# A mixture of experts in blocks: the order of the weight loads, one weight buffer, and where the shared expert's down products stand

## The chip, the cores and the metric

The kernel runs as one program on one core of a Trainium2 chip. The metric is device microseconds from the start of an execution to its end, as the median of several executions. One execution was also profiled; all rows below come from that one.

## The reference, cut to what matters

Two transformer blocks follow each other on 512 tokens of width 1024, in float32. The first block ends in a mixture of experts, and this is where the change lies. Each token goes to 6 of 64 routed experts and also through one shared expert. The result is added to the residual, which the second block norms and projects.

```python
def moe_ffn(h, w_router, b_router, w_exp_gate, w_exp_up, w_exp_down, w_sh_gate, w_sh_up, w_sh_down):
    ...
    def expert_block(xs):
        tok, g, e = xs
        xb = x_pad[tok]
        hb = jax.nn.silu(xb @ w_exp_gate[e]) * (xb @ w_exp_up[e])
        return (hb @ w_exp_down[e]) * g[:, None]
    ...
    shared = (jax.nn.silu(xf @ w_sh_gate) * (xf @ w_sh_up)) @ w_sh_down
    return (shared + routed).reshape(B, S, D)
...
x = x + gate_f * moe_ffn(...)
return rms_norm(x, g_final)        # first_block; second_block begins with rms_norm_2(x, norm_mix) @ w_in
```

A routed expert has three matrices of 1 MB each: gate and up (1024 x 256) and down (256 x 1024). So the 64 experts are 192 MB in all, read once.

## The kernel before, in words

The residual stands in SBUF as `xres` (`xr`), four chunks of 128 tokens. `phase_b` computes the experts. It packs the 64 experts into 32 blocks of 128 token slots (`NB` = 32). A block holds one expert (128 slots), two (96 and 32, or 64 and 64), or three (64, 32, 32); `KINDS` lists the kinds, and `seq` is the order in which blocks are computed. Before the change, counted from block 0, the experts per block in that order are 2 2 2 2 2 3 1 2 2 2 2 3 1 2 2 2 2 3 1 2 2 2 2 3 1 2 2 2 2 3 1 2. The first two blocks (`STAT`) hold fixed experts, whose weights are loaded before the routing is known; the other 60 experts are loaded by an id that the routing gives.

One block is computed in these steps. `expert_h` multiplies the gathered tokens by gate and up on TensorE (PE), and ScalarE (ACT) and VectorE (DVE) make the hidden values `hs` of it (the ACT instruction is at L1011, one for each block). Then the next block's tokens are transposed (`slots_T`, L994), `combine` adds the block before to the residual by products with a selection matrix (L1054, L1055 on PE, the add L1056 on DVE), and `expert_out` multiplies the hidden values by the down matrix (L1033). All blocks cost PE the same, since experts that share a block run beside each other in the array. An optional `slot_info` in some blocks prepares indices of later blocks. Every matrix product of PE on plain float32 stands in the trace as two instructions. GpSimd (POOL) gathers the tokens of the block three further on.

The weights come through SyncE's (SP's) queue. Gate and up go into buffers of 1 MB that hold half of one expert's gate and up (`gu`): 3 named `rawh`, 6 named `raw`, 2 named `rawl`, and as a twelfth one `raws` (`last`), which at first holds the shared expert's down matrix `wd`. The down matrix goes into 8 buffers of 512 KB (`whi`, `wlo`, `rawd`). A buffer is free again when `expert_h` (gate and up) or `expert_out` (down) of its block is through. Each load is a piece of 512 KB: two for a gate-and-up half, one for a half of a down matrix. SP works its queue in order, so a load that waits for a buffer holds back all that stand behind it.

The order of SP's queue is a list that Python writes out, `stream`. `free` is the step at which a load's buffer comes free (step 2i is the end of `expert_h` of block i, step 2i+1 the end of its `expert_out`). Before the change, loads are sorted by `free`, then by the step that needs them.

The shared expert's hidden values `hsT` are made before the loop. Its down products are 4 chunks of tokens, each of 4 products (8 instructions on PE, L1409) and 2 adds on DVE (L1410). Before the change, chunk c stands in block c (`down_at`), ahead of that block's `combine`. When chunk 3 is through, `raws` serves as the twelfth weight buffer.

After the loop, `tail` adds the last two blocks to the residual for chunks 0 and 1, norms these rows (L1449 to L1462), transposes them (L1467), and does the same with chunks 2 and 3. The product of the second block that comes first, `nsa_kv`, multiplies the normed rows by 396 columns of `w_in`. Its matrix is split into high and low parts in four steps `q`, with 3 buffers for each part. Much of the order of instructions on each engine is set by a scheduler, except where `self.chain` or `self.order` ties PE's instructions to each other.

Of the kernel before, what the change touches and what calls it, by code (L numbers as in the profile page):

```python
# [17 lines left out]
OP = mybir.AluOpType  # L18
AX = mybir.AxisListType

T, D, NCH = 512, 1024, 4
KC = D // 128
# [36 lines left out]
class Kern:  # L59
# [861 lines left out]

    def gu(self, h):
        self.turn += 1
        n = self.NP + self.NX + self.NY
        t = self.turn if self.turn < n else (self.turn - n) % (n + 1)
        if t < self.NP:
            return self.hold.tile([128, self.RAW], F32, name="rawh", bufs=self.NP)
        if t < self.NP + self.NX:
            return self.raw(2048)
        return self.spare() if t < n else self.last()  # L930

    def last(self):
        return self.rp.tile([128, self.RAW], F32, name="raws")
# [124 lines left out]
    def phase_b(self):  # L1058
        nc, tc, I = self.nc, self.tc, self.I
        xr, hT, hp = self.xres, self.h2T, self.hp  # L1060
# [6 lines left out]
        wd = self.last().rearrange("p (k n) -> p k n", k=2)  # L1067
# [34 lines left out]
        hsT = rt.tile([128, 2, T], F32, name="hsT")  # L1102
# [11 lines left out]
        for j in range(3):  # L1114
            t = rt.tile([128, D], F32, name=f"xg{j}")
# [5 lines left out]
        p = 0  # L1121
# [75 lines left out]
        p = 0  # L1197
# [6 lines left out]
        for name, src in (("pos", pos), ("gate", sco)):  # L1204
            t = self.tps()
# [4 lines left out]
            t = self.tps()  # L1210
# [58 lines left out]
        seq = ks[0][:]  # L1269
        for i, p in enumerate(ks[2] + ks[3] + ks[5]):  # L1270
            seq.append(p)
            if i % 4 == 2:
                seq += [ks[4].pop(0), ks[1].pop(0)]
        assert sorted(seq) == list(range(NB))


# [1 line left out]
        n = 2  # L1278
# [7 lines left out]

        stream, ngu, ndn = [], self.NP + self.NX + self.NY, self.NHI + self.NLO + self.ND
        ug, ud = [], []  # L1290
        for i, p in enumerate(seq):
            es = self.experts(p)
            for h in range(2):
                for j in es:
                    t = len(ug)
                    free = -1 if t < ngu else 2 * ug[t - ngu] if t < 2 * ngu else 7 if t == 2 * ngu else 2 * ug[t - ngu - 1]
                    ug.append(i)
                    if i >= STAT:
                        stream.append((free, 2 * i, len(stream), p, j, h))
            for j in es:  # L1300
                for k in range(2):
                    t = len(ud)
                    free = -1 if t < ndn else 2 * ud[t - ndn] + 1
                    ud.append(i)
                    if i >= STAT:
                        stream.append((free, 2 * i + 1, len(stream), p, j, 2 + k))
        last = {0: -1, 1: -1}
        for n, (free, *r) in enumerate(stream):
            last[r[-1] > 1] = free = max(free, last[r[-1] > 1])
            stream[n] = (free, *r)  # L1310
        stream.sort()
        ids_of = {}

        def issue(now):

            while stream and stream[0][0] <= now:
                _, _, _, p, j, h = stream.pop(0)
                if (p, j) not in ids_of:
                    ld, (e,) = nc.values_load_multi_w_load_instructions(
                        ids[0:1, j * NB + p:j * NB + p + 1], engines=[mybir.EngineType.SP], min_val=0, max_val=E - 1)  # L1320
                    if len(ends) > 2:
                        self.order(ends[-3], ld[0])
                    ids_of[p, j] = e
                e, w = ids_of[p, j], loads.setdefault(p, {}).setdefault(j, [None] * 4)
                if h < 2:
                    w[h] = self.load_gu(self.gu(h), dyn, e, h)
                else:
                    w[h] = self.load_down(self.down(h - 2), dyn, e, h - 2)
                    ends.append(self.last_load)

        down_at = {0: [0], 1: [1], 2: [2], 3: [3]}
        ends, done = [], []
        fixed_down(1, 1)
        issue(-1)
# [2 lines left out]
                self.run(info(bs))  # L1337
        self.gather(xgs[2], tok[:, seq[2]:seq[2] + 1])
        xT = self.slots_T(xgs[0])
        def overflow():  # L1340

            xo = self.hold.tile([128, self.RAW], F32, name="rawh", bufs=self.NP)
            go, od = [self.spare() for _ in range(2)], self.last()
            more = nc.values_load(late[0:1, n2:], min_val=0, max_val=n2)
            with tc.If(more > 0):
                with tc.For_i(0, more) as q:
                    j = nc.values_load(late[0:1, ds(q, 1)], min_val=0, max_val=n2 - 1)
                    c4 = ep.tile([128, NCH], F32, name="c4")
                    p4 = ep.tile([128, NCH, 6], BF, name="p4")
                    lj = ep.tile([128, 1], F32, name="lj")  # L1350
                    nc.vector.tensor_copy(lj, lim2[:, ds(j, 1)])
                    nc.vector.tensor_copy(c4, slot[:, :, ds(j, 1)].rearrange("p c o -> p (c o)"))
                    nc.vector.tensor_scalar(c4, c4, lj, None, op0=OP.subtract)
                    nc.vector.tensor_copy(p4, pay[:, :, ds(j, 1), :].rearrange("p c o f -> p (c o) f"))
                    ne = nc.values_load(cnt[0:1, ds(j, 1)], min_val=-T, max_val=T)
                    e = nc.values_load(ids[0:1, ds(j, 1)], min_val=0, max_val=E - 1)
                    for b in range(NCH):
                        with tc.If(ne > 128 * b):
                            if b:
                                nc.vector.tensor_scalar(c4, c4, -128.0, None, op0=OP.add)  # L1360
                            o1 = ep.tile([128, 1], I32, name="o_tok")
                            o2 = ep.tile([128, 1], F32, name="o_tokf")
                            o3 = ep.tile([128, 1], F32, name="o_gate")
                            self.run(self.slot_info(ep, 1, [(0, 128, c4[:, :, None], lambda c, j: p4[:, c, :])], (o1, o2, o3)))
                            xg = xo[:, :D]
                            nc.gpsimd.memset(xg, 0.0)
                            self.gather(xg, o1)
                            xT = self.slots_T(xg)
                            w = [self.load_gu(go[h], dyn, e, h) for h in range(2)]
                            w += [self.load_down(od[:, k * D:(k + 1) * D], dyn, e, k) for k in range(2)]  # L1370
                            parts = [(0, 128, w)]
                            hs = self.expert_h(parts, xT, o3, "ho")
                            self.combine([(self.pick(o2), self.expert_out(parts, self.hidden_T(hs)))])
# [9 lines left out]
        for i, p in enumerate(seq):  # L1383
# [16 lines left out]
            if i + 1 < NB:  # L1400
                xT = self.slots_T(xgs[(i + 1) % 3])
                if i + 1 >= NB - 1:
                    nxt = up(xT, seq[i + 1])
            for c in down_at.get(i, []):
                for n in range(2):
                    pd = self.acc()
                    s = slice(n * 512, (n + 1) * 512)
                    for k in range(2):
                        self.pe(nc.tensor.matmul(pd, hsT[:, k, c * 128:(c + 1) * 128], wd[:, k, s], start=(k == 0), stop=(k == 1)))  # L1409
                    nc.vector.tensor_tensor(xr[:, c, s], xr[:, c, s], pd, op=OP.add)  # L1410
            y = None
            if i == NB - 1:
                y = self.hold.tile([128, self.RAW], F32, name="rawh", bufs=self.NP).bitcast(F32R)
# [4 lines left out]
            if done and i < NB - 1:  # L1418
                self.combine(done, range(2, NCH))
                done = []  # L1420
            done.append((self.pick(tokf[:, p:p + 1]), self.expert_out(parts, hT, y)))
            for g in infos:
                self.run(g)
            issue(2 * i + 1)
        self.chain = None
        assert not stream
        g = self.hold.tile([128, self.RAW], F32, name="rawh", bufs=self.NP)
# [3 lines left out]
        nc.gpsimd.tensor_tensor(self.gains[1], self.gains[0], self.gains[1], op=OP.mult)  # L1431

        nc.gpsimd.tensor_tensor(self.gff, self.gains[0], self.gains[0], op=OP.mult)
        self.done, self.ex = done, ex
        bwx.close()

    def tail(self):
# [3 lines left out]
        G = 2  # L1441
        sq2, xn2 = [self.hold.tile([128, self.RAW], F32, name="rawh", bufs=self.NP) for _ in range(2)]
        for a in range(0, NCH, G):
            self.combine(self.done, range(a, a + G))
            st = self.nst[:, a * 6:(a + G) * 6].rearrange("p (s n) -> p s n", s=6)
            xs = [xr[:, a + j, :] for j in range(G)]
            for j in range(G):
# [84 lines left out]
    def phase_c(self):  # L1532
# [66 lines left out]
        def nsa_kv():  # L1599
# [5 lines left out]
            gt = ap.tile([128, 4, 12], F32, name="gt")  # L1605
            raws = [self.load_w(w, 256, N, 4 * h, 4) for h in range(2)]
            ps = [self.acc() for _ in range(NCH)]
            for q in range(4):
                wb = self.split_w(raws[q // 2][:, 2 * (q % 2):2 * (q % 2) + 2], self.fence0 if q >= 0 else None)
                for k in range(2):  # L1610
                    kk = 2 * q + k
                    for c in range(NCH):
                        cc = slice(c * 128, (c + 1) * 128)
                        self.mm3(ps[c][:, :N], hT.hi[:, kk, cc], hT.lo[:, kk, cc], wb.hi[:, k], wb.lo[:, k],
                                 kk == 0, kk == KC - 1)
            for c in range(NCH):
                nc.scalar.activation(kvc[:, c], ps[c][:, 0:128], AF.Copy)
                p4 = ps[c][:, 128:384].rearrange("p (s v d) -> p v s d", s=2, v=2)
# [495 lines left out]
```

## Time and profile before

| | us |
|---|---|
| median of 3 runs | 1771.95 |
| lowest and highest of them | 1765.51, 1772.01 |
| the profiled execution, its own time | 1765.15 |
| its span in the profile | 1763.4 |

The profile names instructions by line and engine, and times are counted from the start of the span. PE, DVE, ACT and POOL are the compute engines, PEld is TensorE's weight load, SPq is SP's queue with the DMA issues, PEclk is the granted TensorE clock as a share of full speed. A bracket at the end of a row gives the time for which the engine stood idle before it, and what released it. Ends on PE are modelled, so the distance between two starts tells more than a duration.

### The profile page before, as it was taken

The numbers are of one execution on the slowest core, as the hardware profiler recorded it, in microseconds if no ns is written. First come the engines' busy times: TensorE is split into PE (matmuls) and PEld (weight loads), VectorE is DVE, ScalarE is ACT, GpSimd is POOL, SyncE is SP. The second block draws the span as 40 slices with busy tenths as digits, with TensorE's granted clock in tenths as the row PEclk, the third lists the DMA queues.
The fourth block names the chain that finished last, engine by engine and source line by source line (L and its number), as shares of the span: only waits on it lengthen the run. The fifth ranks groups of instructions, "written<-read, shape, count | busy, mean of one in ns | idle before, by whom it ended". The sixth has DMA issues, their size and how long they took to land. (4 is left out here: it accounts for less than half of the span.)

```text
span 1763.4 us, 23536 instructions
## 1 busy us (share of the span) xinstructions
PE 1690.5 (96%) x8740; PEld 1130.1 (64%) x8743; DVE 976.9 (55%) x1910; ACT 581.4 (33%) x1112; POOL 69.0 (4%) x107
## 2 busy tenths in 40 slices
PE   7899999999899999899999988999998999999999
PEld 2677766787654444354535437767866788888887
DVE  5585656366846665456546548655455744224422
ACT  3565444423111111111111123454557443114311
POOL 0000000000310000000000010000000000000000
PEclk9999999999999999999999998999999999999999
DMA  9233426138768999999999933201200432233230
GB/s 306 79 121 97 135 96 209 46 114 322 292 264 307 387 408 406 403 403 403 403 396 400 376 135 94 91 19 60 73 24 25 144 96 96 96 96 96 96 119 24
DMA packets 137895, 341.90 MB, mean 194 GB/s; under 512 B 12986, under 2 KB 59389, under 8 KB 137775
## 3 DMA queue, kind: packets, MB, share of 16 engines
q1 hardware_dynamic: 133168, 327.76, 50.7%
q0 software_dynamic: 4608, 12.59, 1.9%
q8 instruction: 71, 1.16, 0.3%
q14 instruction: 48, 0.39, 0.1%
HBM read 340.26 MB, written 4.21 MB: 195 GB/s over the span
## 5 line engine op out<-in xcount | busy, mean ns | idle before, releaser
L89 DVE TENSOR_TENSOR wlo<-raw,whi 128x1024 fp32r<-128x1024 f32 (+4 forms) x162 | 189.6, 1172 | 251.2 <-ACT whi L88 249.6
L88 ACT ACTIVATE whi<-raw 128x1024 fp32r<-128x1024 f32 (+4 forms) x162 | 164.4, 1019 | 253.3 <-PE acc L123 159.9
L1056 DVE TENSOR_TENSOR xres<-xres,acc 128x512 f32<-128x512 f32 x248 | 151.3, 682 | 0.5 <-PE acc L1055 0.5
L1009 PE MATMUL acc<-raw,xT 128*32 128x512 f32 (+2 forms) x704 | 140.2, 602 | 0.0
L121 PE MATMUL acc<-m_hh,whi 128*128 128x512 f32 (+1 forms) x272 | 103.4, 382 | 2.0 <-ACT m_hh L88 2.0
L1054 PE MATMUL acc<-yh,S 128*128 128x512 f32 x248 | 104.5, 421 | 0.0
L123 PE MATMUL acc<-m_hh,wlo 128*128 128x512 f32 (+1 forms) x272 | 103.7, 382 | 0.0
L122 PE MATMUL acc<-m_hl,whi 128*128 128x512 f32 (+1 forms) x272 | 103.7, 382 | 0.0
L88 ACT ACTIVATE yh<-yg 128x512 fp32r<-128x512 f32 x62 | 39.1, 630 | 194.8 <-DVE yg L1035 194.8
L123 PE MATMUL acc<-whi,ul 128*128 128x512 f32 x256 | 101.1, 395 | 0.0
L122 PE MATMUL acc<-wlo,uh 128*128 128x512 f32 x256 | 101.1, 395 | 0.0
L121 PE MATMUL acc<-whi,uh 128*128 128x512 f32 x256 | 101.1, 395 | 0.0
L1033 PE MATMUL acc<-wlo,hT 128*32 128x512 f32 (+2 forms) x312 | 98.9, 642 | 1.1 <-ACT hT L1021 1.1
L1009 PEld LDWEIGHTS acc<-raw,xT 128*32 128x32 f32 (+2 forms) x704 | 48.8, 131 | 79.5 <-issue 72.2
L1012 DVE SCALAR_TENSOR_TENSOR hs<-hs,gate,acc 128x256 f32<-128x256 f32 x32 | 15.4, 480 | 150.1 <-ACT hs L1011 150.1
L1055 PE MATMUL acc<-yl,S 128*128 128x512 f32 x248 | 97.5, 393 | 0.0
L1033 PE MATMUL acc<-whi,hT 128*32 128x512 f32 (+2 forms) x256 | 76.2, 628 | 13.9 <-DMA whi<-in_w_exp_down_dram 12.8
L121 PE MATMUL acc<-hh,whi 128*128 128x512 f32 x192 | 80.9, 421 | 0.0
L123 PE MATMUL acc<-hh,wlo 128*128 128x512 f32 x192 | 76.9, 401 | 0.0
L122 PE MATMUL acc<-hl,whi 128*128 128x512 f32 x192 | 76.9, 400 | 0.0
L1011 ACT ACTIVATE hs<-acc 128x256 f32<-128x256 f32 x32 | 12.3, 384 | 176.8 <-PE acc L1009 176.8
L286 DVE TENSOR_REDUCE st<-s 128x1 f32<-128x128 f32 (+1 forms) x96 | 46.5, 486 | 36.2 <-PE s L324 20.5
(612 smaller groups left out, 3548.3 us busy)
## 6 DMA issues: line engine op xcount, KB each, us to landing
raw<-in_w_exp_gate_dram SPq DMA_DIRECT2D x66, 512.0 KB
raw<-in_w_exp_up_dram SPq DMA_DIRECT2D x66, 512.0 KB
whi<-in_w_exp_down_dram SPq DMA_DIRECT2D x48, 512.0 KB
wlo<-in_w_exp_down_dram SPq DMA_DIRECT2D x48, 512.0 KB
raw<-in_w_in_dram SPq DMA_DIRECT2D x21, 1024.0 KB
rawh<-in_w_exp_gate_dram SPq DMA_DIRECT2D x33, 512.0 KB
rawh<-in_w_exp_up_dram SPq DMA_DIRECT2D x33, 512.0 KB
raw<-in_w_mod_dram SPq DMA_DIRECT2D x16, 1024.0 KB
```

What stands on the lines that cost most here:

```text
L88: self.nc.scalar.activation(hi, src, AF.Copy)
L89: return self.nc.vector.tensor_tensor(lo, src, hi.bitcast(F32), op=OP.subtract)
L121: mm(out, lh, rh, start=start, stop=False)
L122: mm(out, lh, rl, start=False, stop=False)
L123: mm(out, ll, rh, start=False, stop=stop)
L286: nc.vector.tensor_reduce(st[:, 1:2], s_ps[:, :n], axis=AX.X, op=OP.max, negate=True)
L1009: self.pe(nc.tensor.matmul(pg[a:b].rearrange("p (u n) -> p u n", u=2), xT[:, kk, a:b], ws[kk // 4][:, kk % 4], start=(kk == 0), stop=(kk = ...
L1012: nc.vector.scalar_tensor_tensor(hs, hs, gate, pg[:, 256:], op0=OP.mult, op1=OP.mult)
L1033: self.pe(nc.tensor.matmul(p[a:b], hT[:, j, a:b], ws[2 + j][:, s], start=(j == 0), stop=(j == 1)))
L1054: self.pe(nc.tensor.matmul(p, l, y.hi[:, s], start=(i == 0), stop=False))
L1055: self.pe(nc.tensor.matmul(p, l, y.lo[:, s], start=False, stop=(i == len(done) - 1)))
L1056: nc.vector.tensor_tensor(xr[:, c, s], xr[:, c, s], p, op=OP.add)
```

## The change

Five things change. The order of blocks: experts per block are now 2 2 2 2 2 1 3 2 2 1 3 2 2 1 3 2 2 1 3 2 2 1 3 2 2 2 2 2 2 2 2 2, so a block of one expert stands ahead of each block of three. The order of SP's queue: loads are sorted by `at`, which is two blocks ahead of the step that needs them, or `free` if that is later; a load is still written out when its `free` step is past. The twelfth gate-and-up buffer goes: `raws` holds `wd` to the end. The shared down products: chunks 0 and 1 stand in the second and third block of three experts (blocks 10 and 14), behind `combine`; chunks 2 and 3 stand after the loop, between the last sums of chunks 0 and 1 and those of chunks 2 and 3. And `nsa_kv` takes token chunks 0 and 1 through the first three of its four steps `q`, then chunks 2 and 3, then all through the fourth.

```diff
     def gu(self, h):
         self.turn += 1
-        n = self.NP + self.NX + self.NY
-        t = self.turn if self.turn < n else (self.turn - n) % (n + 1)
+        t = self.turn % (self.NP + self.NX + self.NY)
...
-        return self.spare() if t < n else self.last()
+        return self.spare()
...
         for i, p in enumerate(ks[2] + ks[3] + ks[5]):
             seq.append(p)
-            if i % 4 == 2:
-                seq += [ks[4].pop(0), ks[1].pop(0)]
+            if i % 2 == 0 and 2 <= i <= 10:
+                seq += [ks[1].pop(0), ks[4].pop(0)]
...
-                    free = -1 if t < ngu else 2 * ug[t - ngu] if t < 2 * ngu else 7 if t == 2 * ngu else 2 * ug[t - ngu - 1]
+                    free = -1 if t < ngu else 2 * ug[t - ngu]
...
-                        stream.append((free, 2 * i, len(stream), p, j, h))
+                        stream.append((max(free, 2 * i - 4), free, 2 * i, len(stream), p, j, h))
...
-                        stream.append((free, 2 * i + 1, len(stream), p, j, 2 + k))
+                        stream.append((max(free, 2 * i - 3), free, 2 * i + 1, len(stream), p, j, 2 + k))
...
-            while stream and stream[0][0] <= now:
-                _, _, _, p, j, h = stream.pop(0)
+            while stream and stream[0][1] <= now:
+                p, j, h = stream.pop(0)[-3:]
...
-        down_at = {0: [0], 1: [1], 2: [2], 3: [3]}
+        down_at = {i: [c] for c, i in enumerate([i for i, p in enumerate(seq) if len(self.experts(p)) == 3][1:3])}
...
+        def shared_out(c):
+            for n in range(2):
+                pd = self.acc()
+                s = slice(n * 512, (n + 1) * 512)
+                for k in range(2):
+                    self.pe(nc.tensor.matmul(pd, hsT[:, k, c * 128:(c + 1) * 128], wd[:, k, s], start=(k == 0), stop=(k == 1)))
+                nc.vector.tensor_tensor(xr[:, c, s], xr[:, c, s], pd, op=OP.add)
...
-            go, od = [self.spare() for _ in range(2)], self.last()
+            go, od = [self.spare() for _ in range(2)], self.raw(2048)
...
-            for c in down_at.get(i, []):
...
             if done and i < NB - 1:
                 self.combine(done, range(2, NCH))
                 done = []
+            for c in down_at.get(i, []):
+                shared_out(c)
             done.append((self.pick(tokf[:, p:p + 1]), self.expert_out(parts, hT, y)))
...
+        self.combine(done, range(0, 2))
+        for c in range(2, NCH):
+            shared_out(c)
+        self.combine(done, range(2, NCH))
         self.chain = None
...
         for a in range(0, NCH, G):
-            self.combine(self.done, range(a, a + G))
...
-            for q in range(4):
-                wb = self.split_w(raws[q // 2][:, 2 * (q % 2):2 * (q % 2) + 2], self.fence0 if q >= 0 else None)
...
+            wbs = {}
+            for cs, qs in ((range(0, 2), range(0, 3)), (range(2, NCH), range(0, 3)), (range(NCH), range(3, 4))):
+                for q in qs:
+                    if q not in wbs:
+                        wbs[q] = self.split_w(raws[q // 2][:, 2 * (q % 2):2 * (q % 2) + 2], self.fence0)
```

## Rows read from the trace of the kernel before

**Rows 1.** The page: the span.

```profile
span 1763.4 us, 23536 instructions
```

**Rows 2.** Windows, by stretch: busy us (count) by engine, PEclk, DMA share, GB/s.

```profile
550.00:572.00 22.00, 22.00 (x153) 10.28 (x153) 13.88 (x29) 3.23 (x6) 1.98 (x2) 1.00 0.70 261
...
704.00:726.00 22.00, 15.99 (x59) 5.97 (x58) 7.16 (x12) 1.65 (x3) 0.00 (x0) 0.84 1.02 405
...
594.00:946.00 352.00, 339.17 (x1928) 162.01 (x1926) 201.11 (x381) 54.85 (x104) 20.11 (x21) 0.98 1.02 404
```

**Rows 3.** DMA queues of 594 to 946 us: packets, MB, share of 16 engines.

```profile
q1 hardware_dynamic: 36619, 133.35, 95.7%
```

**Rows 4.** Timeline of SP: start, us, the issue (first and last loads by id).

```profile
502.83 0.81 SPq L954 DMA_DIRECT2D rawd<-in_w_exp_down_dram  x2
...
1016.12 0.91 SPq L954 DMA_DIRECT2D rawd<-in_w_exp_down_dram  x2
```

**Rows 5.** Timeline of ACT: L1011 of blocks 0, 11 to 14, 23, 24, 30.

```profile
512.68 0.39 ACT L1011 ACTIVATE hs<-acc 128x256 f32<-128x256 f32 x1 [8.76 <-PE acc L1009]
...
701.45 0.38 ACT L1011 ACTIVATE hs<-acc 128x256 f32<-128x256 f32 x1 [5.17 <-PE acc L1009]
...
726.85 0.38 ACT L1011 ACTIVATE hs<-acc 128x256 f32<-128x256 f32 x1 [5.71 <-PE acc L1009]
...
742.34 0.38 ACT L1011 ACTIVATE hs<-acc 128x256 f32<-128x256 f32 x1 [5.17 <-PE acc L1009]
...
758.53 0.39 ACT L1011 ACTIVATE hs<-acc 128x256 f32<-128x256 f32 x1 [5.63 <-PE acc L1009]
...
905.66 0.38 ACT L1011 ACTIVATE hs<-acc 128x256 f32<-128x256 f32 x1 [5.17 <-PE acc L1009]
...
928.47 0.38 ACT L1011 ACTIVATE hs<-acc 128x256 f32<-128x256 f32 x1 [5.71 <-PE acc L1009]
...
1023.48 0.39 ACT L1011 ACTIVATE hs<-acc 128x256 f32<-128x256 f32 x1 [5.18 <-PE acc L1009]
```

**Rows 6.** Timeline of PE: one undisturbed block, from transposes to transposes.

```profile
843.00 1.23 PE L994 MATMUL t<-ident,xg 128*128 128x128 f32 x8
...
848.08 0.64 PE L1033 MATMUL acc<-wlo,hT 128*64 128x512 f32 x1
...
851.57 3.60 PE L1009 MATMUL acc<-rawl,xT 128*64 128x512 f32 x16
...
858.54 1.23 PE L994 MATMUL t<-ident,xg 128*128 128x128 f32 x8
```

**Rows 7.** Timeline of PE: block 11 waits, then block 12's expert_h.

```profile
713.41 1.06 PE L1033 MATMUL acc<-whi,hT 128*32 128x512 f32 x1 [6.01 <-DMA whi<-in_w_exp_down_dram]
...
719.68 7.13 PE L1009 MATMUL acc<-raw,xT 128*128 128x512 f32 x16
```

**Rows 8.** Source L1409: duration ns min/median/max, first and last start.

```profile
L1409 PE MATMUL acc<-raws,hsT x32: 592/593/595, 513.6 to 573.0; 128*128 128x512 f32 x32
```

**Rows 9.** Timeline, all engines: from the loop's end to the second block.

```profile
1042.09 1.51 SPq L106 DMA_DIRECT2D raw<-in_w_in_dram  x3
...
1043.64 1.57 SPq L152 DMA_DIRECT2D rawh<-in_g_final_dram  x1
...
1053.07 1.90 POOL L1433 TENSOR_TENSOR gff<-rawh 128x1024 f32<-128x1024 f32 x1 [75.25 <-DMA rawh<-in_g_final_dram]
...
1058.56 1.22 DVE L1451 SCALAR_TENSOR_TENSOR rawh<-rawh,gff 128x1024 f32<-128x1024 f32 x1
...
1062.24 0.69 DVE L1056 TENSOR_TENSOR xres<-xres,acc 128x512 f32<-128x512 f32 x1
...
1068.79 1.97 PE L1467 MATMUL t<-ident,rawh 128*128 128x128 f32 x8 [8.12 <-DVE rawh L1462]
...
1078.11 1.03 PE L1467 MATMUL t<-ident,rawh 128*128 128x128 f32 x8
```

**Rows 10.** Windows of the same stretch, columns as in rows 2.

```profile
1061.00:1069.00 8.00, 0.21 (x1) 0.21 (x2) 8.00 (x36) 2.30 (x4) 0.00 (x0) 0.67 0.00 1
```

More of the change, by code (lines that the diff above doesn't have):

```diff
@@ L1305, in phase_b @@
                     if i >= STAT:
-                        stream.append((free, 2 * i + 1, len(stream), p, j, 2 + k))
+                        stream.append((max(free, 2 * i - 3), free, 2 * i + 1, len(stream), p, j, 2 + k))
         last = {0: -1, 1: -1}
-        for n, (free, *r) in enumerate(stream):
-            last[r[-1] > 1] = free = max(free, last[r[-1] > 1])
-            stream[n] = (free, *r)
+        for n, (at, *r) in enumerate(stream):
+            last[r[-1] > 1] = at = max(at, last[r[-1] > 1])
+            stream[n] = (at, *r)
         stream.sort()
@@ L1403, in phase_b @@
                     nxt = up(xT, seq[i + 1])
-            for c in down_at.get(i, []):
[L1405 to L1410, printed above, removed]
             y = None
@@ L1433, in phase_b @@
         nc.gpsimd.tensor_tensor(self.gff, self.gains[0], self.gains[0], op=OP.mult)
-        self.done, self.ex = done, ex
+        self.ex = ex
         bwx.close()
@@ L1607, in nsa_kv @@
             ps = [self.acc() for _ in range(NCH)]
-            for q in range(4):
-                wb = self.split_w(raws[q // 2][:, 2 * (q % 2):2 * (q % 2) + 2], self.fence0 if q >= 0 else None)
[L1610 to L1615, printed above, removed]
+            wbs = {}
[3 more added lines that the diff above has]
+                        wbs[q] = self.split_w(raws[q // 2][:, 2 * (q % 2):2 * (q % 2) + 2], self.fence0)
+                    for k in range(2):
+                        kk = 2 * q + k
+                        for c in cs:
+                            cc = slice(c * 128, (c + 1) * 128)
+                            self.mm3(ps[c][:, :N], hT.hi[:, kk, cc], hT.lo[:, kk, cc], wbs[q].hi[:, k], wbs[q].lo[:, k],
+                                     kk == 0, kk == KC - 1)
             for c in range(NCH):
```

## The prediction

> **What bounds the kernel now.** I looked first at the busy time by slices, to find the stretch that the change touches, then at the windows of that stretch, then at the times of single blocks, and last at the step from the loop to the second block.
>
> The windows show two engines at their limit at once. From 594 to 946 us the DMA engines have a share of 1.02 and move 404 GB/s, and PE is busy for 339 of 352 us [rows 2]. So the loop is a race between loads and products, and what matters is who waits, and where. Early, the loads rest: from 550 to 572 us the share is 0.70 while PE is full [rows 2]. Later, PE waits: of 704 to 726 us it is busy for 15.99, and the timeline shows why, 6.01 us of waiting for a down matrix of block 11, which has three experts [rows 2, 7]. What the loads missed early is paid late.
>
> An undisturbed block lasts 15.54 us (858.54 - 843.00): its `expert_out` begins 5.08 us after the transposes and lasts 3.49, its `expert_h` 6.97 [rows 6]. A block with a `slot_info` lasts 0.65 more (758.53 - 742.34 is 16.19) [rows 5]. A chunk of the shared down products is 8 instructions of the form of which 16 take 7.13 us, less a tail of 0.3, so 3.4 us; the 593 ns of one overlap [rows 7, 8].
>
> So without any waiting, `hs` of block 30 would come at 512.7 + 30 x 15.54 - 3.7 (block 0 has no `combine`: 5.08 less transposes and small work of 1.4) + 12 x 0.65 + 4 x 3.4 = 996.6 us. It comes at 1023.48 [rows 5]. PE loses 26.9 us in the loop: above all at the blocks of three experts, as between 701.45 and 726.85, which is 9.9 over a plain block, or 905.66 to 928.47, 7.3 over [rows 5].
>
> **The loads.** In 352 us the queue brought 133.35 MB, that is 254 pieces of 524,288 bytes, 1.384 us each with the gathers beside them [rows 2, 3]. From 502.83 on 360 pieces are to come (60 experts of 6), so the queue needs 498 us and could be through at 1001. The last pair was issued at 1016.1 and ends near 1019 [rows 4]: the loads rested for some 17 us. The change moves no byte, so 1001 stays the floor.
>
> The Trainium skill's page "DMA: Bandwidth & Descriptors", Specifications, puts the HBM limit of one core at some 358 GB/s. By that figure 360 pieces would take an estimated 527 us, the loads would end at 1030 and nothing could be won. The 404 GB/s of this trace [rows 2] decide against it.
>
> **The change, part by part.**
>
> *Shared chunks out of blocks 0 to 3.* Four times 3.4 us leave the start of the loop, 13.6 us of PE. Two chunks come back in blocks 10 and 14, 6.8 us: net -6.8 on PE. As blocks 0 to 3 end earlier, buffers come free earlier, and the rests around 550 to 572 [rows 2] should shrink. Their 8 adds on DVE move with them; DVE is busy for 201 of 352 us there [rows 2], so in the loop they cost nothing.
>
> *The order of SP's queue.* This adds a wait: gate-and-up loads whose buffer is free after `expert_h` may now stand behind down loads, which wait for that block's `expert_out`, 5.08 + 3.49 = 8.6 us later [rows 6]. Behind the waiting load stands all of SP's queue, and for that the next `expert_h` waits. What hides it is the backlog: for a block of two experts 10 of its 12 pieces can go out at the end of an `expert_out`, 13.8 us of transfer, which is more than 8.6. At the very start there is no such backlog. Of the rests I take half as gone: 17 becomes 9, with bounds of 0 (all gone) and 17 (nothing won).
>
> *One buffer less.* 11 + 4 MB of buffers are 30 pieces, 41.5 us of transfer, where there were 32, 44.3. The loads can run 2.8 us less far ahead; that is inside the bounds just given.
>
> *A block of one expert ahead of each of three.* Three experts are 18 pieces, 24.9 us of loads against 15.5 of PE; one expert is 8.3. Before, the heavy block came first and its loads were late by what rows 7 show. Now the light block gives 7 us of lead. Over four blocks (1, 3, 2, 2 experts) 48 pieces take 66.4 us, and PE takes 62.2, with a shared chunk 65.6: the race stays close, and a little is still lost. I check the worst place by counting. Up to the downs of block 23, with the gate and up of block 24 that stand ahead of them, 272 pieces are to come: 502.8 + 2 (first flight, an estimate) + 9 (rests) + 376.4 = 890. PE's `hs` of block 23 would come at 512.7 + 23 x 15.54 - 3.7 + 10 x 0.65 + 6.8 = 879.7, its `expert_out` 5 us later, with the second half of the downs needed another 1.7 later: 886.4. So some 4 us of waiting remain up to there. After a wait PE runs slow: behind the 6.01 us of waiting, `expert_out` took 6.27 us instead of 3.49, and the granted clock of that stretch is 0.84 [rows 2, 6, 7]. I add 2.8. From block 24 on every block has two experts, 16.6 us of loads against 15.54; the 8 us that the loads fall behind by the end are covered, since by then the queue no longer stands behind another block's gate and up, and the last downs are needed only after `hs` of block 31.
>
> So in the loop PE loses 6.8 us where it lost 26.9. `hs` of block 30 comes at 512.7 + 466.2 - 3.7 + 7.8 + 6.8 + 6.8 = 996.6 instead of 1023.5: **-26.9 us**, of which 20.1 are waits and 6.8 shared products.
>
> *The tail.* Two chunks, 6.8 us of PE, now stand between the sums. Before, PE has nothing to do there: it waits 8.12 us, until 1068.79, for the normed rows [rows 9], so the products are hidden there. If that cover were gone, they would cost 6.8. But DVE is the engine that sets this stretch, busy for 8.00 of 8 us [rows 10], and it gets 4 more adds of 0.65: I take **+3 us**, with the rows of chunks 2 and 3 late. Below: the products keep PE awake, where it now has 0.67 of the clock [rows 10] and takes 1.97 us for 8 transposes that later take 1.03 [rows 9]; two to three such groups won back give -2. Above: +18, the second rival.
>
> *`nsa_kv`.* The trace already has its products on the first rows between the two groups of transposes at 1068.79 and 1078.11 [rows 9], so writing that order out changes nothing; 0, within 1 us, in the tail's bounds. The other buffer in `overflow` stands in a branch that isn't entered.
>
> **The sum.** -26.9 + 3 = -23.9. The span of 1763.4 [rows 1] becomes 1739.5, the profiled execution's 1765.15 becomes 1741.3. Of the four times shown, two lie near 1765 and two 6.8 us higher; I take half of that, 3.4, on top: **1745 us**.
>
> **The rivals.**
>
> *The loads decide.* If PE ends a fixed time after the last load, only the saved rests count: 17 - 9 = 8, less 3 in the tail, -5: 1760 in the profiled execution's terms, 1763 with the 3.4. For it speaks the share of 1.02 through the whole loop [rows 2]. Against it: the last pair was issued at 1016.1, and `hs` of block 30 came only at 1023.5, with block 31 still to be computed [rows 4, 5]; the end was not held by the last piece but by the delay of the heavy blocks before it. Chance 0.15.
>
> *The tail gives it back.* `raws` now holds `wd` until the shared products are through. Should the second block's `w_in` buffers lie on its memory, L106 waits some 23 us longer, and behind it on SP stands the load of the final gain (1042.09, 1043.64); from that to POOL's product it takes 9.4 us, and DVE needs its result at 1058.56 [rows 9]. The gain would be ready at about 1065 + 9.4 + 1.9 = 1076: 18 us late, 15 beyond what I took: 1760. For it: L106 does stand first. Against it: the buffers that L106 gets are freed by the last `expert_h`, so they lie on others. Chance 0.1.
>
> *Slower: SP's queue stands still.* If the backlog doesn't cover the wait behind down loads, each of some 28 blocks costs a rest of the loads. It decides from 23.9 / 28 = 0.85 us for each block; with five pieces queued, 6.9 us, the uncovered part of 8.6 is 1.7 for each block, 48 us in all: 1793. For it: SP's order is strict, and a down load ahead of free gate-and-up buffers is a new wait. Against it: 13.8 against 8.6 us above. Chance 0.07.
>
> *No wait left.* If the loads never rest and PE never waits, 6.8 more are gone and the tail gives -2 instead of 3: 1733. Chance 0.08.
>
> **How the numbers follow.** The forecast has 0.6, and by itself reaches from 1738 (little waiting) to 1754 (rests of before stay in part). The range leaves out the slower case and half of the fastest: 1734 to 1764. Within 0.5% is what a measurement can't tell from no change, here 8.9 us: of the loads' case most falls there (0.12), of the tail's case half (0.05). Faster 0.76, same 0.17, slower 0.07.
>
> **What would show it.** Right: no block of the loop lasts 9 us over a plain one; the DMA share around 550 us is near 1; `hs` of block 30 comes near 997 instead of 1023; in the tail PE has no gap of 8 us. Wrong, if DMA shares fall below 0.9 in the middle of the loop, if the waits only move to block 23 and grow there, or if the step from `hs` of block 30 to the transposes of chunks 2 and 3, 54.6 us before [rows 5, 9], grows by 10.

## The result, and the profile after

The changed kernel takes 1748.45 us (median of 4, 1747.83 to 1756.59) beside 1771.38 of the kernel before: a ratio of 0.9888, 95% interval 0.9853 to 0.9924. That is faster by 1.1%, beyond the 0.5% below which the prediction counts a difference as none, and 3.5 us above the forecast of 1745. Five more executions gave 1751.12 (below, `after_again`). The profiled one took 1748.44, with this span on its page:

```profile
span 1746.4 us, 23495 instructions
```

The timeline of ACT, `hs` of blocks 0, 11, 12, 24, 30 and 31 [rows 5]:

```profile
510.20 0.38 ACT L1010 ACTIVATE hs<-acc 128x256 f32<-128x256 f32 x1 [8.76 <-PE acc L1008]
...
685.97 0.38 ACT L1010 ACTIVATE hs<-acc 128x256 f32<-128x256 f32 x1 [5.43 <-PE acc L1008]
...
702.38 0.38 ACT L1010 ACTIVATE hs<-acc 128x256 f32<-128x256 f32 x1 [5.84 <-PE acc L1008]
...
902.57 0.38 ACT L1010 ACTIVATE hs<-acc 128x256 f32<-128x256 f32 x1 [5.14 <-PE acc L1008]
...
996.25 0.38 ACT L1010 ACTIVATE hs<-acc 128x256 f32<-128x256 f32 x1 [4.96 <-PE acc L1008]
...
1018.02 0.38 ACT L1010 ACTIVATE hs<-acc 128x256 f32<-128x256 f32 x1 [9.11 <-PE acc L1008]
```

From block 0 to block 30 it is now 486.05 us, where it was 510.8 [rows 5]. The windows, columns as in rows 2, show why: PE is busy for 347 of 352 us, and the stretch that had 0.70 of the DMA engines has 0.87.

```profile
550.00:572.00 22.00, 22.00 (x184) 9.68 (x177) 10.66 (x24) 3.04 (x7) 1.98 (x2) 1.00 0.87 334
572.00:594.00 22.00, 22.00 (x111) 12.86 (x111) 16.74 (x34) 3.87 (x8) 1.98 (x2) 1.00 1.03 410
594.00:946.00 352.00, 347.25 (x2030) 166.66 (x2030) 210.88 (x396) 56.34 (x107) 20.77 (x21) 1.00 1.02 404
```

The waits of PE in the loop (us in total, times, longest), first of the kernel before, then of the changed one, and where the longest of these now stands in its timeline:

```profile
PE acc L1033 <- DMA whi<-in_w_exp_down_dram: 12.8, 5, 6.0
```

```profile
PE acc L1032 <- DMA rawd<-in_w_exp_down_dram: 4.8, 4, 2.5
```

```profile
891.45 0.65 PE L1032 MATMUL acc<-rawd,hT 128*64 128x512 f32 x1 [2.48 <-DMA rawd<-in_w_exp_down_dram]
```

Then the stretch behind the loop, all engines [rows 9]: the shared products of chunks 2 and 3 on PE, the load of `w_in` that SP issues behind them, the last add, the norm behind it, the first two groups of transposes, those of chunks 2 and 3.

```profile
1033.07 7.03 PE L1347 MATMUL acc<-raws,hsT 128*128 128x512 f32 x16
...
1040.13 14.25 SPq L106 DMA_DIRECT2D raw<-in_w_in_dram  x4
...
1043.82 0.69 DVE L1055 TENSOR_TENSOR xres<-xres,acc 128x512 f32<-128x512 f32 x1 [0.23 <-PE acc L1054]
1044.42 2.47 DVE L1470 SCALAR_TENSOR_TENSOR rawh<-xres,nst,rawh 128x1024 f32<-128x1024 f32 x2
...
1045.76 1.09 PE L1475 MATMUL t<-ident,rawh 128*128 128x128 f32 x8 [1.98 <-DVE rawh L1470]
...
1048.70 1.97 PE L1475 MATMUL t<-ident,rawh 128*128 128x128 f32 x8 [0.19 <-DVE c_hl L89]
...
1060.24 1.03 PE L1475 MATMUL t<-ident,rawh 128*128 128x128 f32 x8
```

The gap of 8.12 us ahead of the first transposes is gone, but the step from `hs` of block 30 to the last line grew from 54.6 to 64.0. That step overstates the loss, since PE now multiplies the first rows while it waits. A later landmark is better: the pair of `w_in` loads that SP issues in `nsa_kv`'s stage, when PE has run full for 40 us. First before, then after:

```profile
1124.57 21.03 SPq L106 DMA_DIRECT2D raw<-in_w_in_dram  x2
```

```profile
1106.19 21.02 SPq L106 DMA_DIRECT2D raw<-in_w_in_dram  x2
```

So the 17.0 us between the two spans divide like this (`hs` 31 of before comes at 1042.10):

| stretch | before | after | difference |
|---|---|---|---|
| to `hs` 0 (nothing changed) | 512.68 | 510.20 | -2.5 |
| `hs` 0 to `hs` 30, the loop | 510.80 | 486.05 | -24.75 |
| `hs` 30 to `hs` 31 | 18.62 | 21.77 | +3.15 |
| `hs` 31 to the `w_in` pair, the tail | 82.47 | 88.17 | +5.7 |
| from there to the end | 638.8 | 640.2 | +1.4 |

The first and the last line are scatter of unchanged code. The medians of an unchanged kernel scatter by some 4 us from one set of runs to the next (the kernel before: 1767.51 to 1771.38), so the experiments are read by these stretches first. Each stretch is read from one trace; in the five traces that have the changed kernel's loop it lasts 485.6 to 488.3 us, so a difference of 2 or 3 us in the loop is at the edge of what one trace shows. Times in brackets behind a median are the ratio to the kernel before and its 95% interval.

### The profile page after: what moved, and what is told of

Read it like the earlier page. It is cut to its first block, busy times and chain, and to the rows that moved or that the text cites. A ratio compares the mean times of both kernels' runs of the same rounds, so it can differ in the third digit from the quotient of the medians.

```text
span 1746.4 us, 23495 instructions
## 1 busy us (share of the span) xinstructions
PE 1683.9 (96%) x8742; PEld 1131.2 (65%) x8743; DVE 977.9 (56%) x1910; ACT 580.9 (33%) x1112; POOL 68.9 (4%) x107
## 5 line engine op out<-in xcount | busy, mean ns | idle before, releaser
L1008 PE MATMUL acc<-raw,xT 128*32 128x512 f32 (+2 forms) x760 | 148.7, 605 | 0.0
L1011 DVE SCALAR_TENSOR_TENSOR hs<-hs,gate,acc 128x256 f32<-128x256 f32 x32 | 15.4, 480 | 150.0 <-ACT hs L1010 150.0
L1032 PE MATMUL acc<-wlo,hT 128*32 128x512 f32 (+2 forms) x272 | 92.0, 597 | 0.5 <-ACT hT L1020 0.5
L1008 PE MATMUL acc<-rawh,xT 128*32 128x512 f32 (+2 forms) x408 | 83.1, 594 | 0.3 <-ACT xT L998 0.3
```

What stands on the lines that cost most here:

```text
L1008: self.pe(nc.tensor.matmul(pg[a:b].rearrange("p (u n) -> p u n", u=2), xT[:, kk, a:b], ws[kk // 4][:, kk % 4], start=(kk == 0), stop=(kk = ...
L1032: self.pe(nc.tensor.matmul(p[a:b], hT[:, j, a:b], ws[2 + j][:, s], start=(j == 0), stop=(j == 1)))
```

## The experiments

Unless said otherwise, each edits the changed kernel.

**Where the shared chunks belong.** `downs_only` is the kernel before with all four chunks in its first four blocks of three experts, behind `combine`, and with 11 buffers.

```diff
-        down_at = {0: [0], 1: [1], 2: [2], 3: [3]}
+        down_at = {i: [c] for c, i in enumerate([i for i, p in enumerate(seq) if len(self.experts(p)) == 3][0:4])}
...
-        return self.spare() if t < n else self.last()
+        return self.spare()
```

> The kernel before with one part of the change: shared chunks in its four blocks of three experts (5, 11, 17, 23) behind combine, and no twelfth buffer. Block order, queue order and nsa_kv as before. PE has the same work in the loop. Theory A (the shared chunks in blocks 0 to 3 held buffers back, the loads rested there and PE paid at the heavy blocks): the share of the DMA engines at 550 to 572 us rises from 0.70 to above 0.9, the waits of 26.9 us fall to about 10, time about 1754. Rival B (the waits come from the heavy block standing ahead of the light one and from the queue's order): waits stay, time 1771, or a little more for the lost buffer.

1753.84 us (0.9916, 0.9892 to 0.9939); the loop lasts 495.9 us. So 14.9 of the loop's 24.75 us come from this part alone, as theory A had it, although not one product has left the loop: all of it is waits. From 550 to 572 us the DMA share is 1.03. The chunks and the twelfth buffer move together here; no run takes the buffer alone.

`undo_downs` puts the chunks back into blocks 0 to 3, again ahead of `combine`:

```diff
-        down_at = {i: [c] for c, i in enumerate([i for i, p in enumerate(seq) if len(self.experts(p)) == 3][1:3])}
+        down_at = {0: [0], 1: [1], 2: [2], 3: [3]}
...
-        for c in range(2, NCH):
-            shared_out(c)
```

> The changed kernel with the shared chunks back in blocks 0 to 3 ahead of combine; block order, queue order, nsa_kv and the 11 buffers of the change stay. Theory A: the loop gets 6.8 us of PE and about 10 us of waits back, the tail loses its 7, so some 10 above the changed kernel: 1758. Rival B (order of blocks and queue do the work): the loop gets only the 6.8 back and the tail loses 7, so 1748.

1761.39 us (0.9957, 0.9938 to 0.9976), loop 501.4: 15.3 us of the loop are lost again, 6.8 of them the two chunks that come back from the tail, and the DMA shares of the four windows of 22 us from 506 to 594 us are 0.79, 0.86, 0.93 and 0.70, where the changed kernel has 0.95, 1.02, 0.87 and 1.03. Theory A, with 3 us more than its 1758.

`all4_in_threes` takes chunks 2 and 3 out of the tail into two more blocks of three experts:

```diff
-        down_at = {i: [c] for c, i in enumerate([i for i, p in enumerate(seq) if len(self.experts(p)) == 3][1:3])}
+        down_at = {i: [c] for c, i in enumerate([i for i, p in enumerate(seq) if len(self.experts(p)) == 3][1:5])}
...
-        for c in range(2, NCH):
-            shared_out(c)
```

> All four shared chunks stand in the blocks of three experts (10, 14, 18, 22), none behind the loop; the rest is the changed kernel. Theory A (the tail lost 7 us because the second block's w_in loads wait for wd, and PE still waits for weights at blocks 19 and 23, 2.7 and 3.5 us, where 6.8 us of shared products cost nothing): hs of block 30 comes within 1 us of the changed kernel's 996.25, the step from there to the transposes of chunks 2 and 3 falls from 64.0 to about 57, and the time to about 1742. Rival B (the products in the tail were well hidden and the tail is long for another reason, the later branch or the clock): the loop grows by 6.8, the tail stays, 1755.

1747.42 us (0.9881, 0.9855 to 0.9908), and the loop lasts 485.9 us although it holds 6.8 us more of PE's work: the profile has no wait of PE for a load in it any more. The two chunks fill waits that were there anyway. The transposes of chunks 2 and 3 come 35.7 us behind `hs` 31 instead of 42.2. Both are as theory A had them, but its time of 1742 is missed by 5 us: of the 6.5 us that those transposes gain, 3.1 are left at the `w_in` pair (85.0 us behind `hs` 31 instead of 88.2), and `hs` 0 came 2.2 us later in this trace.

**The order of the blocks and of the queue.** `undo_blocks` and `undo_queue` take back one of the two:

```diff
-            if i % 2 == 0 and 2 <= i <= 10:
-                seq += [ks[1].pop(0), ks[4].pop(0)]
+            if i % 4 == 2:
+                seq += [ks[4].pop(0), ks[1].pop(0)]
```

> The changed kernel with the old order of blocks (three experts ahead of one, and further apart); the queue's order, the fifteen gate-and-up buffers and the late shared chunks stay. Theory A: the light block ahead of the heavy one gives the heavy one's loads their lead, so without it PE waits again at the heavy blocks; from the first to the thirty-first hs 492 us instead of 486.05, with waits of 2 us or more behind loads at blocks 23 or 29, and the time 1752 to 1756. Rival B: the lead that the freed PE time at the start gives is enough by itself; 486 within 1.5 us, the time 1748.

1752.11 us (0.9906, 0.987 to 0.9942), loop 490.2: 4.1 us worse, somewhat less than theory A had, and not nothing. PE's longest wait is 2.9 us.

```diff
-                        stream.append((max(free, 2 * i - 4), free, 2 * i, len(stream), p, j, h))
+                        stream.append((free, free, 2 * i, len(stream), p, j, h))
...
-            while stream and stream[0][1] <= now:
+            while stream and stream[0][0] <= now:
```

> The changed kernel with SP's queue sorted as before, each load at the moment its buffer is free. Theory A: the loads stay near 400 GB/s whichever of them goes first, and the order of the queue is worth at most 3 us; hs 0 to hs 30 lasts 486 to 489 us, the time 1746 to 1752. Rival B: loads needed later take the transfer time of those needed now, and PE waits at the heavy blocks; 494 us or more, the time 1756 or more.

1751.75 us (0.9913, 0.9886 to 0.994), loop 491.6: 5.6 us worse, 2.6 above what theory A allowed for the loop and 2.4 below what rival B asked for; the time is within theory A's 1746 to 1752. The new order does cost early rests (the share from 550 to 572 us is 1.03 here, 0.87 with it) and gives more back later. With `downs_only` the parts sum up: 14.9 + 4.1 + 5.6 = 24.6 us of the loop's 24.75. That they meet so closely is partly chance, by the spread of 485.6 to 488.3.

**The tail.** In the changed kernel SP holds the first load of `w_in` until the shared products have read `wd`, as a rival had feared. `wd_apart` gives `wd` a buffer that nobody waits for:

```diff
-        wd = self.last().rearrange("p (k n) -> p k n", k=2)
+        wd = rt.tile([128, self.RAW], F32, name="wd").rearrange("p (k n) -> p k n", k=2)
```

> The changed kernel with wd in another pool of the same side, so that the buffers of the second block's first w_in loads no longer lie on it; nothing else differs. Theory A (the tail's 6.8 us beyond the branch come from w_in's loads, which wait until the shared products are through, and their splits land in the middle of the norm): w_in is issued when expert_h of block 31 is through, some 22 us earlier, the step from hs of block 30 to the transposes of chunks 2 and 3 falls from 64.0 to about 59 or 60, time about 1744. Rival B (the four adds on DVE and the order of its work make the tail long): step and time stay, 1748.

1751.92 us (0.9909, 0.988 to 0.9938). The timeline of SP shows the load 21 us earlier, at 1019.08, and yet the transposes of chunks 2 and 3 stand 42.7 us behind `hs` 31, as before it:

```profile
1019.08 1.50 SPq L106 DMA_DIRECT2D raw<-in_w_in_dram  x3
```

```profile
1061.75 1.03 PE L1475 MATMUL t<-ident,rawh 128*128 128x128 f32 x8
```

So theory A falls: the late load costs nothing. The windows point to DVE as what sets the tail. In the changed kernel DVE (third of the busy times) works for 13.0 of 15 and 16.3 of 17 us, though in the first of the two PE (first) is busy for 12.9 as well; no run takes work off DVE alone:

```profile
1030.00:1045.00 15.00, 12.90 (x41) 7.67 (x41) 12.98 (x33) 3.83 (x7) 3.08 (x2) 1.00 0.26 87
1044.00:1061.00 17.00, 12.25 (x54) 10.92 (x55) 16.26 (x33) 5.69 (x10) 0.00 (x0) 0.70 0.50 167
```

`undo_kv` has the loop of `nsa_kv` as before:

```diff
-            for cs, qs in ((range(0, 2), range(0, 3)), (range(2, NCH), range(0, 3)), (range(NCH), range(3, 4))):
+            for q in range(4):
...
-                        for c in cs:
+                    for c in range(NCH):
```

> The changed kernel with the loop of nsa_kv written as before. Theory A: the products on the first rows were already put between the two groups of transposes; the transposes of chunks 2 and 3 come 42 us behind the last hs as now, and from there to the end it lasts 685 to 693 us as in the other runs; 1748 within 3 us. Rival B: the written-out order saves time behind those transposes; the step from there to the gathers of nsa_kv's result grows by 3 us or more and the time with it, 1751 or more.

By the trace theory A: `hs` 31 to the `w_in` pair takes 87.8 us beside 88.2. The median does not show it: 1756.17 (0.992, 0.9894 to 0.9947), a time as rival B had it. Three executions gave 1750.1 to 1751.5 (the trace is of one of them) and four 1756.2 to 1759.0, with a mean granted clock of 0.983 or 0.984 instead of 0.986 to 0.989. What the four lost is not in the trace. The kernel before, run beside it, splits in the same way without this edit (nine executions from 1762.7 to 1767.5, eight from 1772.0 to 1776.2), so the split is no sign of the loop's order.

**The branch.** Ahead of block 31's transposes stands the branch of `overflow`, which isn't entered. PE's gap there grew from 4.16 us to 6.79, and with it the step from `hs` 30 to `hs` 31. Before, then after:

```profile
1031.71 1.95 PE L994 MATMUL t<-ident,xg 128*128 128x128 f32 x8 [4.16 <-DVE S L1042]
```

```profile
1007.12 1.95 PE L993 MATMUL t<-ident,xg 128*128 128x128 f32 x8 [6.79 <-PEq L1355]
```

`all4_late` is `all4_in_threes` with the last four down loads behind the branch on SP:

```diff
+                    if i == NB - 1:
+                        free = 2 * i - 2
```

> All four shared chunks in blocks of three experts, and the four down loads of the last block issued two half blocks later on SP, which puts them behind the branch for overflowing slots. Theory A: the branch waits until SP has come past the loads queued ahead of it, and that is the 3.1 us by which hs 30 to hs 31 grew; it falls from 21.8 to about 18.8, and the time by some 3 us, to 1744. Rival B: that gap has another cause (the products or the clock at the loop's end); it stays at 21.8, or the later loads make it longer, and the time is 1747 or more.

1746.29 us (0.9872, 0.9843 to 0.99), and `hs` 30 to `hs` 31 is 18.96. The step is theory A's, and the time lies between its 1744 and the rival's 1747. But the mechanism of theory A fell with another run: in `undo_queue` SP had passed its own branch 8.6 us ahead of PE (1000.8, 1009.4), and PE's branch was long all the same; two loads of gains, issued at 1008.95, were in flight there. The view by source line gives PE's branch instruction itself (ns; start). In `undo_queue`, in the kernel before, and in the changed one:

```profile
L1355 SPq COMPARE_BRANCH  x1: 58/58/58, 1000.8 to 1000.8; - x1
L1355 PEldq COMPARE_BRANCH  x1: 5672/5672/5672, 1009.4 to 1009.4; - x1
```

```profile
L1345 PEldq COMPARE_BRANCH  x1: 3332/3332/3332, 1027.7 to 1027.7; - x1
```

```profile
L1355 PEldq COMPARE_BRANCH  x1: 6012/6012/6012, 1000.5 to 1000.5; - x1
```

What goes with it is the load on the DMA engines meanwhile. While the branch of the kernel before runs, the DMA queues move nothing but this:

```profile
q8 instruction: 1, 0.02, 1.8%
q14 instruction: 1, 0.01, 0.6%
```

In each of the twelve traces with the branch, exactly one packet of q8 runs during it. Cut to 0.1 us, it runs 0.9 to 1.4 us behind the start of the branch in the five short ones and 2.5 to 3.5 us behind it in the seven long ones, and the branch ends 2.3 to 2.7 us later in all twelve. First the kernel before, 1028.7 to 1028.8 us, then the changed one, 1004.0 to 1004.1, 1.0 and 3.5 us behind the start:

```profile
q8 instruction: 1, 0.02, 59.9%
```

```profile
q8 instruction: 1, 0.02, 69.3%
```

So what grows is the time until this packet runs. The reading is that it carries PE's instructions behind the branch and comes later beside loads; the trace doesn't name the engine that q8 serves. Over the branch in these twelve traces:

| kernel | DMA share during it | PE's branch, us | `hs` 30 to 31, us |
|---|---|---|---|
| before; `downs_only` | 0.02; 0.02 | 3.33; 3.31 | 18.62; 18.78 |
| `undo_blocks` | 0.12 | 3.79 | 18.89 |
| `all4_late`; `late_only` | 0.17; 0.24 | 3.81; 3.67 | 18.96; 19.30 |
| `undo_kv`; `undo_queue` | 0.60; 0.62 | 5.35; 5.67 | 20.25; 20.66 |
| `undo_downs` | 0.71 | 4.95 | 19.94 |
| `after_again`; after | 0.84; 0.86 | 5.95; 6.01 | 21.74; 21.77 |
| `wd_apart`; `all4_in_threes` | 0.87; 0.93 | 5.75; 5.85 | 21.75; 21.83 |

The Trainium skill's page "Runtime: NRT & Kernel Launch", Instruction fetch mechanics, says that a taken branch whose target isn't among the pages already fetched forces a DMA fetch of that page before execution can go on. The one packet of q8 in each of these traces agrees; one of q14 doesn't run in all of them (none in `all4_late` and `late_only`).

`late_only` makes that edit alone in the changed kernel, `no_branch` leaves the branch out as well, and `after_again` is the changed kernel once more, on the same chip.

> The changed kernel, and of it only the four down loads of the last block issued two half blocks later, behind the branch for overflowing slots. In ten traces PE's branch instruction there lasts 3.3 us with the DMA engines idle and 5.0 to 6.0 us with the last loads in flight. Theory A: nothing is in flight when PE comes to the branch now, so it lasts 3.3 to 4 us instead of 6.01, hs 30 to hs 31 falls from 21.8 to about 19, and the time by some 2.5 us, to 1746 in executions without a dip of the clock. Rival B: the branch costs what it costs for another reason; 21.8 and 1748.5.

1747.89 us (0.9886, 0.9866 to 0.9905); PE's branch lasts 3.67 us, and `hs` 30 to `hs` 31 19.30 instead of 21.77. Theory A; the median is 3.2 us below that of `after_again`, run beside it, though not below the first median of the changed kernel.

> The changed kernel without the branch for overflowing slots, and with the late down loads of late_only; the part of the computation behind the branch, which isn't entered with these inputs, is left out. Theory: the whole price of the branch is PE's gap of 6.8 us, the transposes of the next block at half the clock behind it (1.95 against 1.23 us) and the block's first products at half the clock; hs 30 to hs 31 becomes that of a plain block, 15.5 us, and the time 1740 to 1743. Rival: the last block waits for its late down loads, or the clock falls elsewhere; 18 us or more, and 1745.

1743.98 us (0.9867, 0.9844 to 0.9891). Without the branch the transposes of block 31 stand ahead of `hs` 30, so the step is taken from block 29: `hs` 29 to `hs` 31 is 28.8 us where it was 37.3. So without the branch, and with the late loads, the changed kernel gains 8.5 us there: the 6.79 of the gap and the clock behind it. Block 31's products take 7.11 us here at a granted clock of 1.00, and 8.96 in the changed kernel, where the clock is 0.50 from 1007 to 1009 us and 0.52 from there to 1013. The time is a little above what the theory had.

> The changed kernel once more, unaltered, for the scatter of its executions. Theory A: its times fall into two groups, near 1748 with a mean granted clock of 0.986 or more, and 6 to 8 us above with 0.984 or less, and a trace of the second group differs from one of the first by a stretch near 1140 us at half the clock. Rival: the times spread evenly between 1746 and 1758, and the clock doesn't tell them apart.

1751.12 us (0.9904, 0.9887 to 0.9921), all five from 1750.45 to 1752.39. Both expectations miss: no second group, and no wide spread. The trace repeats the stretches: loop 486.6, `hs` 30 to 31 21.74, tail 87.9.

## Why the prediction was right, and where it was not

The sum was -26.9 in the loop and +3 in the tail, to a span of 1739.5. The span is 1746.4. Of the 6.9 us between them the loop has 2.15, the branch 3.15, the tail 2.7, scatter of unchanged stretches -1.1.

*The loop.* It was to last 996.6 - 512.7 = 483.9 us, and lasts 486.05 (485.6 to 488.3 in the five traces with the same loop). `hs` 30 stands at 996.25 as forecast only because the stages ahead were 2.5 us quicker. The steps hold: no block is 9 us over a plain one, loads run at 404 GB/s, and the longest wait left is at the downs of block 23, the place counted out as the worst, with 2.48 us of the "some 4". The prediction left 6.8 us for waits and slow clock. The waits alone sum to 4.8; with the clock behind them it is some 7.0, since `all4_in_threes`, which waits for no load, takes 485.87, and less its two more chunks 479.1. So the remaining waits were sized right, and what is 2 us short is the sum of PE's plain work (483.9 - 6.8 = 477.1 for 479.1). One sign of being right did not come: the DMA share around 550 us is 0.87 and not near 1.

*Which part does it.* The text gave 6.8 us to the shared products and 20.1 to the waits, but did not divide the waits among the edits. The runs do: moving the shared products out of blocks 0 to 3 is 15 us, even where all four stay in the loop (`downs_only`), since it lets the loads run early; the order of the queue is 5.6, the order of the blocks 4.1. The new wait on SP is there (0.87 for 1.03), and the backlog covers it from 572 us on.

*Net -6.8 on PE* was counted as a gain, and it is none: `all4_in_threes` keeps these products in the loop and lasts as long (485.87 for 486.05). The loop is a race, and there PE's time is free wherever PE would wait.

*The tail.* +3 became +5.7. The step from `hs` 30 to the transposes of chunks 2 and 3, a sign of being wrong if it grew by 10, grew by 9.4, 3.15 of it by the branch. The term that was named, four adds on DVE and the late rows, was about right: `all4_late` and `late_only` differ by the place of these two chunks alone, and take 84.3 and 88.0 us from `hs` 31 to the `w_in` pair, so 3.7. But `undo_downs`, which has no chunk in its tail either, takes 87.0; by that trace it is 1.2. Another 0.9 to 4.5 us come with the tail's new code even where no chunk stands in it (84.3, 85.0 and 87.0, beside 82.5 and 83.3 with the old one). Why is open. That the products keep PE awake shows in the first group of transposes (1.09 us for 1.97) and is gone in the second (1.97).

*What was missing:* the branch. An earlier end of the loop brought PE to it while the last loads were in flight, +3.15 us. The prediction had the last loads and `hs` 30 in its rows, but no price for the branch between them.

*The rivals.* "The tail gives it back" saw the held `w_in` load rightly (the waits of SP show 29.8 us for L1347) and priced it wrongly at 15: `wd_apart` shows 0. Its chain needed the load of the final gain to stand behind the held load on SP, but in the changed kernel that load is issued at 1009.38, some 31 us ahead of it. "The loads decide" fell: the loop kept the gain. `nsa_kv` at 0 holds by the trace. The profiled execution's 1748.44 is 7.1 us above the 1741.3 that the sum gave for it. That the median comes within 3.5 us of the forecast is due to the 3.4 us added for scatter, and that is luck: nine executions of the changed kernel lie between 1747.83 and 1756.59.

*What beats both, by this stretch:* `all4_late`. From `hs` 0 to the `w_in` pair it takes 589.1 us (511.74 to 1100.81) where the changed kernel takes 596.0 and the kernel before 611.9; its lowest time is 1743.88, its median 1746.29. The medians alone don't tell it from the changed kernel: the intervals of the ratios overlap (0.9843 to 0.99 and 0.9853 to 0.9924).

## What to carry to other kernels

Where loads and products race, take work off PE where its delay keeps buffers occupied, and put it where PE waits for a load: here four chunks, 13.6 us of PE, were moved within the loop, and that was worth 15 us of waits. Before work goes into a gap at a loop's end, ask which engine sets that stretch; while PE stood idle there, DVE was busy for 8.00 of 8 us. When a stage ends earlier, look at what its end now meets: here a branch met the last loads.

## What the runs showed of the hardware

A branch that isn't entered costs PE 3.3 us with the DMA engines idle (share 0.02) and up to 6.0 beside loads (0.86). Leaving it out of the changed kernel gives 8.5, with the products behind it, which ran at half the clock (0.50) at first. An instruction packet, one in each trace, ran 1.0 us behind the branch's start in the first case and 3.5 in the second.

In `all4_late` the granted clock fell toward its lower level (1.2 of 2.4 GHz) in a later stage, where PE had been busy for 10.95 of 13 us; the changed kernel had the same busy time ahead of the same stage and kept the full clock. From there to the next load of `w_in` it took 35.4 us (1138.58 to 1174.03) instead of 30.1 (1143.23 to 1173.34); `wd_apart` shows the same. The windows of `all4_late`, then of the changed kernel:

```profile
1125.00:1138.00 13.00, 10.95 (x54) 6.22 (x54) 8.29 (x23) 7.07 (x23) 0.00 (x0) 0.96 0.01 3
1138.00:1156.00 18.00, 18.00 (x72) 11.08 (x71) 7.97 (x24) 5.49 (x16) 0.00 (x0) 0.65 0.01 1
```

```profile
1130.00:1143.00 13.00, 10.95 (x58) 6.35 (x56) 8.52 (x23) 7.23 (x22) 0.00 (x0) 1.00 0.04 14
1143.00:1158.00 15.00, 14.64 (x86) 9.58 (x85) 8.21 (x25) 5.95 (x17) 0.00 (x0) 1.00 0.01 2
```

So a part of the scatter between executions can come from this stage, which no experiment touched; how much, the runs do not show.
